# Loads of tiles 2 to 5 on the stores' DMA queue, in a kernel that scales every row by two weights

## The chip, the cores and the metric

The kernel runs on one core of a Trainium2 chip. The metric is the device time of one execution in microseconds (us); a kernel is run several times and the median is given. A profile is one further execution, recorded by the hardware profiler. DVE is VectorE, ACT is ScalarE, SP is SyncE, POOL is GpSimd. SP and ACT each have a DMA queue; both queues are served by the core's 16 DMA engines.

## What is computed

Each of 16 x 1024 tokens has a row of 512 floats and two weights. The output holds the row twice, each time multiplied by one of the weights:

```python
batch, seq, hidden, n_experts = 16, 1024, 512, 8     # k = 2
x_expanded = x[:, :, np.newaxis, :].repeat(k, axis=2)
weights = expert_weights[..., np.newaxis]
return (x_expanded * weights).astype(np.float32)
```

`expert_indices` is not used. 33.6 MB are read and 67.1 MB written.

## The kernel before

The 16384 tokens are cut into six tiles: five of 24 tokens for each of the 128 partitions, and one of 8 (`groups`, L33). In a tile, a partition holds successive tokens, so a load of a large tile is 128 rows of 48 KB (6144 KB), and tile 5's load is 2048 KB. `x_pool` has two buffers for loaded tiles, and so load i needs the buffer of tile i - 2. The output of a tile is made in halves of 12 tokens (`TO`), each in one of two buffers of `o_pool` and stored with one DMA of 6144 KB (L137). The text calls the two stores of tile i "ia" and "ib"; tile 5 has only one store, of 4096 KB.

The loop at L93 goes over the tiles. Of each six tokens of a half, four are multiplied by one DVE instruction (L121, 128 x 4096) and two by four ACT instructions (L104, 128 x 512 each). The first half of tile 0 is different: it is done row by row (L110 on DVE, L104 on ACT), because tile 0 is loaded in six chunks of four tokens (L81) so that work can start early.

`load(i)` (L75) issues the DMA of a tile. Loads 0 and 1 are issued ahead of the loop; load i + 2 is called at the end of the loop's turn for tile i (L141), so in program order it stands right behind that tile's last store. The stores are all issued from SP (L137). Which engine issues a load is chosen at L83: SP for the last tile, ACT for all others. An engine works through its program in order, and a DMA issue first waits for the semaphores it needs: a store for DVE and ACT to have written its half, a load for both engines to have read the old tile out of its buffer. The framework adds the semaphore waits; each DMA has one of eight completion semaphores in rotation, and it may also wait for the earlier transfer that used the same one. The weights (L54 to L60) come in three small loads on SP at the start.

Of the kernel before, what the change touches and what calls it, by code (L numbers as in the profile page):

```python
# [1 line left out]

# [4 lines left out]


@with_exitstack
def kernel(  # L10
    ctx: ExitStack,
    tc: tile.TileContext,
    x: bass.AP,
    expert_indices: bass.AP,
    expert_weights: bass.AP,
    out: bass.AP,
):
    nc = tc.nc

    batch, seq, hidden = x.shape  # L20
    k = expert_weights.shape[-1]
    P = nc.NUM_PARTITIONS
    ntok = batch * seq
    assert ntok % P == 0
    A_TOTAL = ntok // P

    f32 = mybir.dt.float32
    row = k * hidden
    TX = 24
    TO = 12  # L30
    CH = 4

    groups = [[24], [24], [24], [24], [24], [8]]  # L33
    assert sum(sum(g) for g in groups) == A_TOTAL

    xf = x.rearrange("b s h -> (b s) h")
    of = out.rearrange("b s k h -> (b s) (k h)")
    wf = expert_weights.rearrange("b s k -> (b s) k")

    w_pool = ctx.enter_context(tc.tile_pool(name="w_pool", bufs=1))  # L40
    x_pool = ctx.enter_context(tc.tile_pool(name="x_pool", bufs=2))
    o_pool = ctx.enter_context(tc.tile_pool(name="o_pool", bufs=2))

    w_tile = w_pool.tile([P, A_TOTAL * k], f32)

    def rows(of_all, done, T):
        return of_all[done * P : (done + T) * P, :].rearrange(
            "(p a) n -> p (a n)", a=T
        )

    T0 = sum(groups[0])
    G = len([g for g in groups[1:] if sum(g) == T0])
    head = (1 + G) * T0
    nc.sync.dma_start(out=w_tile[:, : T0 * k], in_=rows(wf, 0, T0))  # L54
    nc.sync.dma_start(
        out=w_tile[:, T0 * k : head * k].rearrange("p (g n) -> p g n", g=G),
        in_=wf[T0 * P : head * P, :].rearrange("(g p a) n -> p g (a n)", g=G, p=P),
    )
    nc.sync.dma_start(
        out=w_tile[:, head * k :], in_=rows(wf, head, A_TOTAL - head)  # L60
    )

    tiles = []
    done = 0
    for group in groups:
        T = sum(group)
        a0 = 0
        for n in group:
            tiles.append((done, T, a0, n))
            a0 += n  # L70
        done += T

    loaded = []

    def load(i):  # L75
        if i >= len(tiles):
            return
        done, T, a0, n = tiles[i]
        x_tile = x_pool.tile([P, TX * hidden], f32)
        src = rows(xf, done, T)  # L80
        step = TX // 6 if i == 0 else n  # L81

        queue = nc.sync if i == len(tiles) - 1 else nc.scalar  # L83
        for at in range(0, n, step):
            queue.dma_start(
                out=x_tile[:, at * hidden : (at + step) * hidden],
                in_=src[:, (a0 + at) * hidden : (a0 + at + step) * hidden],
            )
        loaded.append(x_tile)

    for i in range(2):
        load(i)
    for i, (done, T, a0, n) in enumerate(tiles):  # L93
        x_tile = loaded[i]
        outr = rows(of, done, T)
        for t in range(n):
            if t % TO == 0:
                o_tile = o_pool.tile([P, TO * row], f32)
            single = i == 0 and t < TO
            for kk in range(k if single or t % TO % 6 > 3 else 0):  # L100
                c = (done + a0 + t) * k + kk
                o = t % TO * row + kk * hidden
                if not single or c % 3 == 2:
                    nc.scalar.mul(  # L104
                        out=o_tile[:, o : o + hidden],
                        in_=x_tile[:, t * hidden : (t + 1) * hidden],
                        mul=w_tile[:, c : c + 1],
                    )
                    continue
                nc.vector.tensor_scalar(  # L110
                    out=o_tile[:, o : o + hidden],
                    in0=x_tile[:, t * hidden : (t + 1) * hidden],
                    scalar1=w_tile[:, c : c + 1],
                    scalar2=None,
                    op0=mybir.AluOpType.mult,
                )
            if not single and t % TO % 6 == 0:
                c = (done + a0 + t) * k
                o = t % TO * row
                m = min(CH, n - t)  # L120
                nc.vector.tensor_tensor(  # L121
                    out=o_tile[:, o : o + m * row].rearrange(
                        "p (t k h) -> p t k h", t=m, k=k
                    ),
                    in0=x_tile[:, t * hidden : (t + m) * hidden]
                    .rearrange("p (t h) -> p t h", t=m)
                    .unsqueeze(2)
                    .to_broadcast([P, m, k, hidden]),
                    in1=w_tile[:, c : c + m * k]
                    .rearrange("p (t k) -> p t k", t=m)  # L130
                    .unsqueeze(3)
                    .to_broadcast([P, m, k, hidden]),
                    op=mybir.AluOpType.mult,
                )
            if (t + 1) % TO == 0 or t + 1 == n:
                at = t // TO * TO
                nc.sync.dma_start(  # L137
                    out=outr[:, (a0 + at) * row : (a0 + t + 1) * row],
                    in_=o_tile[:, : (t + 1 - at) * row],
                )  # L140
        load(i + 2)  # L141

# [1 line left out]
_INS = ['x', 'expert_indices', 'expert_weights']  # L144
_OUTS = [((16, 1024, 2, 512), 'float32')]


# [23 lines left out]
```

## Time and profile before

| | |
|---|---|
| median of 3 runs | 240.34 us (240.26 to 242.69) |
| the profiled execution | 240.03 us, of which its span 238.1 us |
| DVE busy | 92.2 us (39%) |
| ACT busy | 54.2 us (23%) |
| moved by DMA | 100.80 MB, mean 423 GB/s over the span |
| large loads from ACT's queue | 4 of 6144 KB and 6 chunks of 1024 KB |
| stores from SP's queue | 10 of 6144 KB, 1 of 4096 KB |

The span runs from the first instruction to the last; the execution's own time has some 1.9 us around it. The profile cuts the span into 40 slices, and a digit is the busy share of a slice in tenths. An issue row of a DMA gives the time from issue to landing, that is until the last of its data has arrived and the semaphore is complete. A DMA queue on an engine is written SPq or ACTq. Row counts of x1 in the issue rows are single transfers, from the issues of a short stretch of time.

In the chain of work that ended last, stores hold 50% of the span, DVE's L121 18%, and loads 12%. The issue times of the kernel before: the stores 0b at 32.75, 1a 66.26, 1b 80.45, 2a 107.94, 2b 129.99, 3a 146.37, 3b 173.49, 4a 187.99, 4b 202.65 and 5 at 219.88 us; the loads 2 at 32.76, 3 at 80.47 and 4 at 130.01 us from ACT, and 5 at 173.92 us from SP.

### The profile page before, as it was taken

Reading aid. Unit: us, or ns where it says so; the run is one execution under the profiler, and the core shown is the slowest. Engines: PE = TensorE matmul, PEld = TensorE weight load, DVE = VectorE, ACT = ScalarE, POOL = GpSimd, SP = SyncE. Lnnn points to the kernel's source line nnn. Section 1 sums busy time; section 2 is a strip of 40 time slices with the busy share of each in tenths; the row PEclk is TensorE's granted clock in tenths of the full one; section 3 lists DMA queues with packets and bytes.
Section 4 is the critical chain, followed back from the end, with each engine's and each line's share of the span. In section 5 each row is a group of like instructions: output and inputs, shape, how many; then the busy total and the mean of one; then the engine's idle time right before and its main releaser. Section 6 shows DMA issues by size and latency. Waiting matters only on the chain.

```text
span 238.1 us, 232 instructions
## 1 busy us (share of the span) xinstructions
DVE 92.2 (39%) x36; ACT 54.2 (23%) x85; POOL 0.2 (0%) x4
## 2 busy tenths in 40 slices
DVE  0890240003919500391068085003919549019000
ACT  0841210003408000340061080003408044012000
POOL 0000000000000000000000000000000000000000
DMA  6998999999999999999999999999999999999996
GB/s 246 423 441 362 516 413 396 429 495 396 396 504 421 396 421 504 396 398 495 429 396 413 504 405 396 479 446 396 413 495 413 396 416 465 405 495 421 396 440 264
DMA packets 3986, 100.80 MB, mean 423 GB/s; under 512 B 1169, under 2 KB 1169, under 8 KB 1169
## 3 DMA queue, kind: packets, MB, share of 16 engines
q1 hardware_dynamic: 2544, 69.34, 67.5%
q10 hardware_dynamic: 1440, 31.46, 31.2%
q14 instruction: 2, 0.01, 0.0%
HBM read 33.69 MB, written 67.11 MB: 423 GB/s over the span
## 4 chain that ended last, share of the span: by engine, by line
DMA 62%; DVE 18%; another core or an unknown queue 10%; DVEq 1%; issue 0%; SPq 0%
DMA out_dram<-o_tile 50%; DVE o_tile L121 18%; DMA x_tile<-in_x_dram 12%; DVEq L166 1%; DVEq L121 0%; SPq L137 0%
## 5 line engine op out<-in xcount | busy, mean ns | idle before, releaser
L121 DVE TENSOR_TENSOR o_tile<-x_tile,w_tile 128x4096 f32<-128x4096 f32 (+1 forms) x20 | 85.6, 4316 | 121.0 <-DMA out_dram<-o_tile 85.7
L104 ACT ACTIVATE o_tile<-x_tile,w_tile 128x512 f32<-128x512 f32 x84 | 52.9, 709 | 155.0 <-DMA out_dram<-o_tile 115.8
L110 DVE TENSOR_SCALAR o_tile<-x_tile,w_tile 128x512 f32<-128x512 f32 x16 | 6.6, 483 | 6.6 <-DMA x_tile<-in_x_dram 6.6
L104 ACT ACT_TABLE_LOAD x1 | 1.3, 1283 | 6.6 <-DMA x_tile<-in_x_dram 6.6
L155 POOL MEMSET const-bfloat16-1.0<- 128x1 bf16 x1 | 0.1, 101 | 0.0
L155 POOL MEMSET const-uint8-127<- 128x1 uint8 x1 | 0.1, 101 | 0.0
L155 POOL MEMSET const-float32-0.0<- 128x1 f32 x1 | 0.1, 98 | 0.2 <-issue 0.2
L155 POOL MEMSET const-float32-1.0<- 128x1 f32 x1 | 0.1, 98 | 0.0
## 6 DMA issues: line engine op xcount, KB each, us to landing
out_dram<-o_tile SPq DMA_DIRECT2D x10, 6144.0 KB, 31.0
x_tile<-in_x_dram ACTq DMA_DIRECT2D x4, 6144.0 KB, 42.2
x_tile<-in_x_dram ACTq DMA_DIRECT2D x6, 1024.0 KB, 10.5
out_dram<-o_tile SPq DMA_DIRECT2D x1, 4096.0 KB, 17.4
x_tile<-in_x_dram SPq DMA_DIRECT2D x1, 2048.0 KB, 24.6
w_tile<-in_expert_weights_dram SPq DMA_DIRECT2D x1, 96.0 KB, 11.2
w_tile<-in_expert_weights_dram SPq DMA_DIRECT2D x1, 24.0 KB, 3.4
w_tile<-in_expert_weights_dram SPq DMA_DIRECT2D x1, 8.0 KB, 13.3
```

The lines of the kernel that those rows point to most:

```text
L104: nc.scalar.mul(out=o_tile[:, o : o + hidden], in_=x_tile[:, t * hidden : (t + 1) * hidden], mul=w_tile[:, c : c + 1],)
L110: nc.vector.tensor_scalar(out=o_tile[:, o : o + hidden], in0=x_tile[:, t * hidden : (t + 1) * hidden], scalar1=w_tile[:, c : c + 1], scala ...
L121: nc.vector.tensor_tensor(out=o_tile[:, o : o + m * row].rearrange("p (t k h) -> p t k h", t=m, k=k), in0=x_tile[:, t * hidden : (t + m) * ...
L155: nc = _bacc.Bacc("TRN2", target_bir_lowering=False, num_devices=1)
L166: with _tile.TileContext(nc) as tc:
```

## The change

Loads 2, 3 and 4 are issued from SP instead of from ACT, as load 5 already is. In SP's program each stands right behind the second store of the tile two before it, whose x buffer it takes. ACT's queue keeps the six chunks of tile 0 and the load of tile 1.

```diff
-        queue = nc.sync if i == len(tiles) - 1 else nc.scalar
+        queue = nc.sync if i >= 2 else nc.scalar
         for at in range(0, n, step):
             queue.dma_start(
```

Built, ACT's program loses three DMA issues and SP's gains them; SP's order becomes two stores, load, two stores, load, and so on. DVE's program has the same instructions in the same order.

## The prediction

> **What bounds the kernel now.** I read the page's table of slices first, then the DMA queues, then busy time by window, then the waits, then the single transfers.
>
> ```profile
> DMA  6998999999999999999999999999999999999996
> DMA packets 3986, 100.80 MB, mean 423 GB/s; under 512 B 1169, under 2 KB 1169, under 8 KB 1169
> q1 hardware_dynamic: 2544, 69.34, 67.5%
> q10 hardware_dynamic: 1440, 31.46, 31.2%
> ```
>
> The 16 DMA engines are 90% busy or more in nearly every slice. Only the first slice and the last are clearly lower. Packet time adds up to 67.5 + 31.2 = 98.7% of 16 engines' span: no spare DMA time exists, and the compute engines (DVE 39%, ACT 23%) are far from a bound. q10 is ACT's queue (the five large loads, 31.46 MB), q1 is SP's.
>
> The windows tell whether the mixture of loads and stores matters (columns: stretch, length, busy time and count for DVE, ACT and POOL, TensorE clock, DMA share, GB/s):
>
> ```profile
> 30.00:113.80 83.80, 28.97 (x7) 15.84 (x26) 0.00 (x0) 1.00 1.00 432
> 113.80:130.00 16.20, 8.76 (x2) 5.01 (x8) 0.00 (x0) 1.00 1.01 437
> 130.00:162.70 32.70, 8.76 (x2) 5.01 (x8) 0.00 (x0) 1.00 1.00 433
> 174.00:234.00 60.00, 24.15 (x6) 12.58 (x20) 0.00 (x0) 1.00 1.00 434
> 174.00:200.00 26.00, 14.93 (x4) 10.02 (x16) 0.00 (x0) 1.00 1.02 440
> ```
>
> In 30 to 113.8 and 130 to 162.7 a load on ACT's queue runs beside stores on SP's; in 113.8 to 130 there are stores alone; from 174 on, everything already sits in SP's one queue, with tile 5's load between two stores. The rate is 432 to 437 GB/s in all of them. What sets the time is therefore the bytes, and the DMA engines must merely never run out of queued work.
>
> ```profile
> ACT o_tile L104 <- DMA out_dram<-o_tile: 115.8, 8, 22.5
> DVE o_tile L121 <- DMA out_dram<-o_tile: 85.7, 8, 18.7
> DVE o_tile L121 <- DMA x_tile<-in_x_dram: 35.4, 3, 24.8
> ```
>
> DVE waits mostly for a store to give its o_tile back; it waited for loads three times only, and those are tiles 0 and 1.
>
> The issue rows by window give landing times, in order tile 0's second store, load 2, store 3b, load 5:
>
> ```profile
> out_dram<-o_tile SPq DMA_DIRECT2D x1, 6144.0 KB, 38.8
> x_tile<-in_x_dram ACTq DMA_DIRECT2D x1, 6144.0 KB, 51.8
> out_dram<-o_tile SPq DMA_DIRECT2D x1, 6144.0 KB, 20.2
> x_tile<-in_x_dram SPq DMA_DIRECT2D x1, 2048.0 KB, 24.6
> ```
>
> ```profile
> 173.92 0.82 SPq L85 DMA_DIRECT2D x_tile<-in_x_dram  x1
> 187.99 32.22 SPq L137 DMA_DIRECT2D out_dram<-o_tile  x3
> ```
>
> Store 3b is issued at 173.49 and lands at 173.49 + 20.2 = 193.7. Load 5, from SP, is issued at 173.92, so it did not wait for that store, and lands at 198.5, 4.8 us behind it. From there to the last landing (219.88 + 17.4 = 237.3) 18 MiB of load 5, stores 4a, 4b and 5 pass in 43.6 us: 14.53 us for each 6144 KB, or 433 GB/s. This is the unit of what follows.
>
> **The change, part by part.** Loads 2, 3 and 4 move from ACT's queue to SP's; load 5 was there and stays. No byte, arithmetic instruction or tile changes.
>
> *ACT loses three DMA issues* of 0.37, 0.36 and 0.35 us (1.08 us). ACT idles 155.0 us, so the gain on the path is 0.
>
> *SP gains three issues.* Load 5 shows 0.82 us for one issued right behind a store: 3 x 0.82 = 2.5 us. SP's stores wait 201.8 us for DVE in all, and the next store is over 25 us away in each case, so this is covered: 0. Without that cover it would be +2.5 us.
>
> *Waits on SP.* A load needs both engines to have finished with its x_tile; the store just ahead of it in SP's program waits for those same last instructions, so nothing new is waited for there. In the built program's list of waits, load 2 waits for tile 0's chunk loads, load 3 for load 1, load 4 for load 2 and store 0a, load 5 for load 3 and store 1a. All of these have landed long before by the schedule below. Queued behind the waiting load is the next tile's first store, which is not ready until later anyway. 0.
>
> *Order in the queue.* This is the real change: a load no longer shares the engines with stores but takes its turn. Up to 57.24 us (load 1 landed, the chain's row for L121 at 57.43) nothing differs, as load 2 sat behind load 1 so far. In the kernel before, store 0b then shared half the rate with load 2 until 32.75 + 38.8 = 71.5; alone it needs half of those 14.3 us and lands near 64.4. Counted backwards from 237.3 by bytes (11 units and 14.5 us for load 5 and store 5, 174.3 us) it is 63.0. I use 63.0, the one with less slack. Landings then follow each other by 14.53: load 2 at 77.5, store 1a 92.1, 1b 106.6, load 3 121.1, 2a 135.6, 2b 150.2, load 4 164.7, 3a 179.2, 3b 193.8, load 5 198.6, 4a 213.1, 4b 227.7, store 5 237.3. Before, 3a landed at 146.37 + 32.7 = 179.1: from there on both schedules are the same.
>
> Is each transfer issued before the one ahead of it ends? Half a tile takes 8.77 us on DVE (two of L121) plus about 0.1 us of issue. Store 1a is issued at 66.3 as before, 11.2 us before load 2 ends. Half 1b no longer waits for store 0b: issue at 75.0, 17 us ahead, and load 3 right behind it, 31 us ahead. Half 2a starts when 1a lands (92.1), issue 101.0 against 121.1: 20 us. Half 2b: 115.5 against 135.6. Half 3a: 144.5 against 164.7. Half 3b: 159.1 against 179.2. Half 4a: 188.1 against 198.6; 4b: 202.7 against 213.1; store 5: 219.8 against 227.7, 7.9 us. That smallest slack is in the kernel before too (219.88 against 202.65 + 24.9 = 227.6). The queue never empties, so the stall removed is 0 and the stall added is 0.
>
> *Loads landing later.* Load 3 lands at 121.1 instead of 80.47 + 33.3 = 113.8, load 4 at 164.7 instead of 162.7. Their tiles' first halves wait for a store's o_tile until 135.6 and 179.2, so 14.5 us of cover remain. DVE's waits just change length.
>
> *The turn from store to load inside one queue* is six times new. Between bounds: in the mixed stretches packets of both kinds alternate throughout, at 433 against 437 GB/s for stores alone; charged wholly to the turns, 0.9% of a 48 KB packet (128 rows of 48 KB over 16 engines are 8 packets, 14.53 / 8 = 1.8 us) is 0.02 us each, 0.1 us in sum. The other end is the 440 of 174 to 200, the very pattern in one queue: over the 117 us from 63 to 180 it would save 117 x 7 / 440 = 1.9 us. Its DMA share is 1.02, though, and 440 / 1.02 = 431: whole packets counted at the window's edge. I take 0.
>
> The Trainium skill's page "DMA: Bandwidth & Descriptors", section "Issuing engines are not separate DMA queues", says that transfers started from different engines run on the same 16 DMA engines and only issue time is saved by spreading them. By that rule the sum is 0 as well, and the rates by window agree. A rule that speaks against the change is in "Perfetto Trace Analysis" of the Trainium skill, section "DMA Optimizations": give inputs one issuing engine and outputs another, for a more dynamic spread. It is priced as the second rival; the 434 GB/s from 174 on, with both kinds in one queue, does not bear it out.
>
> **Sum.** 238.1 us span + 0 = 238.1; the profiled execution's own time is 240.03, 1.9 us more than its span, and the median of the runs shown is 240.34, 0.3 above it. Against that median: 240.3 us.
>
> **Rivals.**
>
> 1. *SP stalls at a load (slower).* If a load's issue had to wait for the store ahead of it to land, the one queue would run dry each time. The small 24 KB weight load shows 3.4 us from issue to landing, mostly start-up. Three or four such holes are +10 to +14 us, near 252. It decides where the awaited transfer lands later than the queue's last one. Against it: load 5 was issued 0.43 us after store 3b in the trace, 19.8 us before that landed, and the list of waits above names only old transfers.
> 2. *Head-of-line blocking (slower).* A finished first-half store stands behind a load in the queue, its o_tile comes back late, and a half's computing (8.8 us) is exposed in three tiles: up to +26 us, near 266. It decides once a store's issue is later than the end of the load ahead, that is when 11 to 20 us of slack are gone. Against it: 1a lands at 92.1 rather than at 66.26 + 32.7 = 99.0, since it no longer shares.
> 3. *One kind at a time is really quicker.* 240.3 - 1.9 = 238.4, from the 440 GB/s row; still within 1%. Over 1% would take 2.4 us, and the DMA share of 1.00 in the mixed stretches leaves no idle time to win. Against it as above.
>
> **How the numbers follow.** No change 0.87; rival 1 0.05; rival 2 0.03; rival 3 0.05, of which 0.02 over 1%. So faster by over 1% (which is about what a measurement of this kernel can tell from no change) 0.02, within 1% 0.87 + 0.03 = 0.90, slower 0.05 + 0.03 = 0.08. The range need not reach to the rivals, which hold 0.13. Low end: 434 instead of 432 GB/s over 117 us is -0.5 us, from the profiled 240.03: 239.5. High end: the turns' 0.1 us and the scatter, one of three runs at 242.69; half way from the median to it is 241.5.
>
> **What would show it.** Right: DMA 9 in all slices but the first and last; ACT's queue at 12.58 MB instead of 31.46; loads 2 to 4 issued within 1 us behind a second store, at about 33, 76 and 116, and load 5 at 160; load 3 landing near 121; 3a onward as before; a rate of 432 to 437 in each window; DVE's waits for loads still three. Wrong: a slice with DMA at 8 or less between 60 and 180 us, an SP load whose issue comes near the landing of the store ahead of it (rival 1), DVE waiting for x_tile beyond tile 1 or a store issued after its predecessor has landed (rival 2), or a longer steady rate near 440 (rival 3).

## The result, and the profile after

| | before | after |
|---|---|---|
| median of 20 runs | 240.36 us (239.88 to 243.5) | 242.17 us (240.21 to 243.01) |
| ratio of the times | | 1.0048, 95% interval 1.0026 to 1.007 |
| the profiled execution | 240.03 us, span 238.1 | 242.16 us, span 240.2 |

The change costs about half a per cent: 0.0048 x 240.36 = 1.15 us, between 0.6 and 1.7. The medians lie further apart (1.8 us) because both kernels scatter over about 3 us: of the 20 runs, 4 of the kernel before and 11 of the changed one are above 242 us. The two profiled executions, 2.1 us apart, show what separates such runs: that of the kernel before is one of its quickest, that of the changed kernel lies at its median.

The page of the changed kernel, with the DMA share by slice and the queues:

```profile
DMA  7999999999999999999999999999999999999993
DMA packets 3985, 100.80 MB, mean 420 GB/s; under 512 B 1168, under 2 KB 1168, under 8 KB 1168
q1 hardware_dynamic: 2976, 88.21, 85.4%
q10 hardware_dynamic: 1008, 12.58, 12.8%
```

The loads moved as written (ACT's queue q10 has 12.58 MB left), and no slice in the middle falls below 9. Only the last slice tells anything: 3 where it was 6. The windows of the changed kernel, with the columns as before:

```profile
30.00:113.80 83.80, 35.50 (x9) 20.59 (x33) 0.00 (x0) 1.00 1.00 431
130.00:162.70 32.70, 17.52 (x4) 10.02 (x16) 0.00 (x0) 1.00 1.00 433
174.00:234.00 60.00, 24.15 (x6) 12.58 (x20) 0.00 (x0) 1.00 1.00 431
```

The mean rate is at most 3 GB/s lower than in the same windows of the kernel before. The loss must be looked for in single transfers. Their issue rows in the changed kernel, one short window each, in this order: store 0b (issued at 32.48), load 2 (33.01), store 1b (74.67), load 3 (75.05), stores 2a (101.17) and 2b (115.75), load 4 (116.17), stores 3a (145.57) and 3b (160.01), load 5 (160.43), store 4a (189.71). Store 1a, between load 2 and store 1b, is left out. The last column is the time from issue to landing.

```profile
out_dram<-o_tile SPq DMA_DIRECT2D x1, 6144.0 KB, 30.7
x_tile<-in_x_dram SPq DMA_DIRECT2D x1, 6144.0 KB, 44.7
out_dram<-o_tile SPq DMA_DIRECT2D x1, 6144.0 KB, 32.1
x_tile<-in_x_dram SPq DMA_DIRECT2D x1, 6144.0 KB, 47.0
out_dram<-o_tile SPq DMA_DIRECT2D x1, 6144.0 KB, 35.4
out_dram<-o_tile SPq DMA_DIRECT2D x1, 6144.0 KB, 35.3
x_tile<-in_x_dram SPq DMA_DIRECT2D x1, 6144.0 KB, 50.1
out_dram<-o_tile SPq DMA_DIRECT2D x1, 6144.0 KB, 35.2
out_dram<-o_tile SPq DMA_DIRECT2D x1, 6144.0 KB, 35.3
x_tile<-in_x_dram SPq DMA_DIRECT2D x1, 2048.0 KB, 40.2
out_dram<-o_tile SPq DMA_DIRECT2D x1, 6144.0 KB, 25.5
```

Issue plus landing gives 63.2, 77.7, 106.8, 122.1, 136.6, 151.1, 166.3, 180.8, 195.3, 200.6, 215.2. So from one landing to the next: load 2 14.5 us, load 3 15.3, 2a 14.5, 2b 14.5, load 4 15.2, 3a 14.5, 3b 14.5, load 5 5.3, 4a 14.6. Every store takes 14.5 or 14.6, and so does load 2, which loses nothing. Loads 3 and 4 take 0.8 and 0.7 more, and load 5, of a third of the size, 0.5 more than its 4.8 in the kernel before. These three come to 2.0 of the 2.1 us between the two executions.

A landing is the last of 16 DMA engines. How far apart they are is seen at the very end, when nothing is queued any more. The kernel before (windows of 1 us):

```profile
235.00:236.00 1.00, 0.00 (x0) 0.00 (x0) 0.00 (x0) 1.00 1.06 459
236.00:237.00 1.00, 0.00 (x0) 0.00 (x0) 0.00 (x0) 1.00 0.01 0
```

and the changed kernel:

```profile
235.00:236.00 1.00, 0.00 (x0) 0.00 (x0) 0.00 (x0) 1.00 1.21 524
236.00:237.00 1.00, 0.00 (x0) 0.00 (x0) 0.00 (x0) 1.00 0.23 98
237.00:238.00 1.00, 0.00 (x0) 0.00 (x0) 0.00 (x0) 1.00 0.15 66
```

A packet counts in the window where it starts. In both kernels most engines begin their last packet before 236 us. Store 5's packets have 32 KB (4096 KB in 128 rows). In the changed kernel three of them begin between 236 and 237 us (98 GB/s for 1 us) and two between 237 and 238 (66). Most engines are as early as ever; a few are 1 to 2 us late, and the kernel waits for them.

The packet records of the two traces, which the views above only sum up, tell where those engines fall behind. Each trace has 1792 packets of 48 KB, and nearly all take 1.82 us. Over 0.1 us longer take 6 in the kernel before and 25 in the changed kernel. Of these 25, 14 begin from 118.1 to 119.4 us, in the last 4 us of load 3, and four from 162.7 to 163.6, in the last 4 us of load 4. The other seven begin in the first 5 us of loads 2, 3 and 4. So packets stretch near the places where loads and stores meet, most of them near the end of a load that has a store behind it.

### The profile page after: what moved, and what is told of

It is laid out like the page before. It is cut to its first block, busy times and chain, and to the rows that moved or that the text cites. A ratio compares the mean times of both kernels' runs of the same rounds, so it can differ in the third digit from the quotient of the medians.

```text
span 240.2 us, 237 instructions
## 1 busy us (share of the span) xinstructions
DVE 92.1 (38%) x36; ACT 54.2 (23%) x85; POOL 0.2 (0%) x4
## 3 DMA queue, kind: packets, MB, share of 16 engines
q10 hardware_dynamic: 1008, 12.58, 12.8%
## 4 chain that ended last, share of the span: by engine, by line
DMA 62%; DVE 18%; another core or an unknown queue 10%; DVEq 1%; issue 0%; SPq 0%
DMA out_dram<-o_tile 51%; DVE o_tile L121 18%; DMA x_tile<-in_x_dram 11%; DVEq L166 1%; DVEq L121 0%; SPq L137 0%
## 5 line engine op out<-in xcount | busy, mean ns | idle before, releaser
L104 ACT ACTIVATE o_tile<-x_tile,w_tile 128x512 f32<-128x512 f32 x84 | 52.9, 709 | 157.1 <-DMA out_dram<-o_tile 118.1
```

The costliest lines, as they stand in the source:

```text
L104: nc.scalar.mul(out=o_tile[:, o : o + hidden], in_=x_tile[:, t * hidden : (t + 1) * hidden], mul=w_tile[:, c : c + 1],)
```

## Experiments

Theory A said that a load which has the DMA engines to itself loses time on some of them, because no other queue's packets fill in; B, that reading by all engines at once loses time whatever the queues; C, that the turn between loads and stores inside one queue does; D, that it is an issue or arithmetic going on during the load; N, that it was chance.

**The changed kernel again**, unaltered.

> The changed kernel once more, unaltered, for a second trace. In the first trace load 3, load 4 and load 5 took 15.3, 15.2 and 5.4 us from the landing ahead of them, where stores of the same size took 14.5. Theory A (a load that has the DMA engines to itself loses time on a few engines, because no other queue's packets fill in): loads 2 to 4 together take 44.6 to 46 us between landings, the stores 14.5 each, time 0.3 to 0.9% above the kernel before. Theory C (the cost is of the turns from store to load in a queue): much the same. Rival N (chance, a disturbance of that one execution): loads 14.5 to 14.6 as well, time within 0.2% of the kernel before.

Measured 242.84 us, ratio 1.0061 (1.0036 to 1.0086). N falls. In this trace, too, all the stores behind load 2 take 14.5 or 14.6 us, while loads 3 and 4 take 15.4 and 16.0 and load 5 takes 5.1; load 2 takes 14.6. At the end the DMA share is 0.31, 0.08 and 0.15 in the windows from 236, 237 and 238 us.

**Loads alone and stores alone.** The edit is shortened here; one small store follows the loads.

```diff
+    for i in range(14):                      # x_pool with three buffers
+        x_tile = x_pool.tile([P, TX * hidden], f32)
+        queue = nc.sync                      # second: nc.scalar if i % 2 else nc.sync
+        queue.dma_start(out=x_tile[:, :], in_=rows(xf, i % 5 * TX, TX))
```

> Left out: weights, arithmetic and all stores but one small one. 14 loads of 6144 KB from SP's queue alone, three buffers, so that two further loads are always queued. 14 x 14.53 = 203.4, and with the start and the small store some 208 us of span if loads run like stores. Theory A (loads alone lose for want of a second queue): 4 to 10 us more than that, 0.3 to 0.7 per load. Theory B (reading alone by all engines at once loses time, whatever the queues): 4 to 10 us more as well. Theory C (turns from store to load cost): nothing more, within 1 us of 14.53 each.

> Left out: as in the kernel with loads from one queue. The same 14 loads, alternately from SP's and ACT's queue, so that mostly two are in flight at once. Theory A: 3 us or more shorter than from one queue, near 208 us of span. Theory B: as long as from one queue, within 1.5 us. Theory C: near 208 us, like one queue.

> Left out: all loads and the arithmetic; two filled buffers are stored 14 times with 6144 KB each from SP's queue. All theories: 14.5 us for each, 203 us and the start (filling the buffers, some 10 to 15 us): the measure of a transfer that loses nothing.

Loads from one queue took 212.06 us (span 210.4), from two queues 212.00 (210.2), stores 221.55 (219.8). The span of the loads is 2 us above the 208 forecast without a loss, short of the 4 to 10 that A and B expected, and the two kernels differ by 0.06 us. In one queue each load from the second on lands 14.5 us after the one ahead of it. The rate of loads in one queue, and then that of stores:

```profile
30.00:205.00 175.00, 0.00 (x0) 1.00 1.00 433
```

```profile
30.00:205.00 175.00, 0.00 (x0) 0.00 (x0) 1.00 1.00 431
```

Loads among loads lose no more than stores among stores. So A and B fall: it takes loads and stores together.

**Turns in one queue**, with nothing else. Two filled buffers are stored and loads go to buffers that nobody reads; only the order differs (the edit is shortened). In the built program the first load stands ahead of the first store, as the expectations write the order.

```diff
+    for what in "SSL" * 5:                   # then "S" * 10 + "L" * 5, then "SL" * 7
+        if what == "S":
+            nc.sync.dma_start(out=outr[:, ...], in_=o_tiles[stores % 2][:, :])
+        else:
+            queue.dma_start(out=x_tile[:, :], in_=rows(xf, loads % 5 * TX, TX))
```

> Left out: weights and arithmetic; two filled buffers are stored and loads go to buffers that nobody reads. Ten stores and five loads of 6144 KB, all from SP's queue, in the order L SS SS L SS L SS L SS L: eight turns between loads and stores. Theory C (a turn within one queue costs the slower engines some time; the changed kernel's two traces give 0.6 us for the two turns of a load, from 1.5 to 1.6 us for the three large ones and 0.3 to 0.6 for load 5): 1.8 us more than the kernel with two turns (6 x 0.3). Theory D (what costs is an issue or arithmetic going on during the load): the same time as with two turns, within 0.4 us.

> Left out: as above. The same ten stores and five loads from SP's queue, in the order L, ten S, four L: two turns. All theories: 14.5 us for each transfer between landings, and the span of the other less what six turns cost.

> Left out: weights and arithmetic, as in the kernels with eight and two turns. Seven stores and seven loads of 6144 KB, all from SP's queue, in the order L S S L S L S L S L S L S L: twelve turns, five loads in the middle and one at the end with stores ahead but none behind. Without any price of a turn the last landing is at 20.5 + 13 x 14.5 = 209.1 us. Theory C, as a price of each turn from load to store (the kernel with eight turns lost 0.2 to 0.7 at each of three middle loads and nothing at its last one): the five middle loads take 14.7 to 15.2 between landings, the last one 14.5, the last landing is at 210.1 to 212.6. If each turn from store to load costs too, the last load takes over 14.7 as well. Rival N (chance): all 14.5 to 14.6.

Measured 227.16 us with eight turns, 226.21 with two, 213.44 with twelve (that one moves one transfer less). With the same transfers, three more loads between stores cost 227.16 - 226.21 = 0.95 us, or 0.32 each, about half of the 1.8 us that C had forecast; the four runs of each kernel lie from 226.95 to 227.59 and from 225.31 to 226.37. For twelve turns the two-turn kernel less one transfer gives 226.21 - 14.5 = 211.7; the 1.7 us above it are 0.35 for each of five loads between stores. The issue rows with eight turns: the second store of the second pair (issued at 27.59), the first load between stores (28.32), the next store (29.05), the one after (29.78), the next load (30.53):

```profile
out_dram<-o_tile SPq DMA_DIRECT2D x1, 6144.0 KB, 50.7
x_tile<-in_x_dram SPq DMA_DIRECT2D x1, 6144.0 KB, 65.0
out_dram<-o_tile SPq DMA_DIRECT2D x1, 6144.0 KB, 78.9
out_dram<-o_tile SPq DMA_DIRECT2D x1, 6144.0 KB, 92.7
x_tile<-in_x_dram SPq DMA_DIRECT2D x1, 6144.0 KB, 106.6
```

Landings at 78.3, 93.3, 108.0, 122.5, 137.1: the first load takes 15.0 us, the second 14.6, the stores 14.5 to 14.7. With twelve turns the end is instructive: the last load between stores (issued at 122.90), a store (123.29), and the last load, which has a store ahead and nothing behind (152.30):

```profile
x_tile<-in_x_dram SPq DMA_DIRECT2D x1, 6144.0 KB, 58.4
out_dram<-o_tile SPq DMA_DIRECT2D x1, 6144.0 KB, 72.6
x_tile<-in_x_dram SPq DMA_DIRECT2D x1, 6144.0 KB, 58.0
```

Landings at 181.3, 195.9 and 210.3: the last load takes 14.4 us. In the two-turn kernel the loads behind the last store take 14.5 each (180.1, 194.6, 209.1, 223.6). So a load behind a store loses nothing as such; one that has a store behind it loses 0 to 1.2 us, differently each time (the five with twelve turns take 15.3, 15.7, 14.5, 14.9, 14.5). The first load of the two-turn kernel gives way to a store too. It lands at 20.5 us, the first of the loads alone at 18.6: 1.9 us, so the 0.32 and 0.35 are means and not a fixed price. C holds, as a price of the place where a load gives way to a store. D falls: while the loads between stores ran, there was no arithmetic, and SP issued nothing.

**More and fewer turns in the kernel.** First the x tiles in halves, so that a load of 3072 KB stands behind each store:

```diff
-    x_pool = ctx.enter_context(tc.tile_pool(name="x_pool", bufs=2))
+    x_pool = ctx.enter_context(tc.tile_pool(name="x_pool", bufs=4))
...
-        load(i + 2)
+                load(i + 2, t // TO)         # behind each half's store
```

> The changed kernel with the x tiles cut in two: a load of 3072 KB stands behind each first store and each second store, so the moved bytes are the same and the turns in SP's queue are twice as many for loads 2 to 4. Theory C: its loss over the kernel before is about double that of the changed kernel, 1.0% against 0.5% (near 242.7 against 241.5 where the kernel before has 240.3). Theory D (issues during a load) and any price per byte loaded: like the changed kernel, 0.3 to 0.7%.

Measured 243.03 us, ratio 1.008 (1.0049 to 1.011). That is 1.9 us for six loads between stores, 0.32 each: C's side, though the interval reaches down to 0.5% and so does not exclude by itself the 0.3 to 0.7% of D and of a price per byte.

Then load 5 on ACT's queue as well, and load 3 alone on SP's:

```diff
-        queue = nc.sync if i >= 2 else nc.scalar
+        queue = nc.scalar                    # second: nc.sync if i in (3, 5) else nc.scalar
```

> The kernel before with load 5, too, on ACT's queue: no queue turns any more. Theory C: nothing lost at load 5, whose two turns cost the kernel before next to nothing in its trace (4.8 us between landings): 0 to 0.2% below the kernel before. Rival (more mixing costs): slower by up to 0.3%.

> The kernel before with load 3 alone moved to SP's queue; loads 2 and 4 stay on ACT's. Theory C: load 3 stands between stores 1b and 2a in one queue and takes 15.0 to 15.4 us between landings; time 0.1 to 0.3% above the kernel before. Rival N (chance, or a cost of something else in the change): load 3 takes 14.5 to 14.6; the time as before, within 0.1%.

Measured 241.04 us, ratio 0.9987 (0.9955 to 1.0019), and 242.22 us, ratio 1.0017 (0.9986 to 1.0048). Both are too small for their intervals: they agree with 0.3 to 0.4 us for a load, and with nothing. In the second, load 4 from ACT's queue runs into the end of load 3, so that load 3's landing says nothing either.

Then the moved loads in four DMAs each, in the kernel and in the queue of eight turns:

```diff
-        step = TX // 6 if i == 0 else n
+        step = TX // 6 if i == 0 else n // 4 if i >= 2 else n
```

> The changed kernel with each moved load cut into four DMAs of a quarter of the row (12 KB rows for loads 2 to 4, 4 KB for load 5), the turns in SP's queue as many as before. If the price goes with the packet that is under way at the turn (48 KB, 1.8 us): a quarter of the loss, 0.1 to 0.3% above the kernel before. If it goes with the turn itself: 0.4 to 0.7% as for the changed kernel.

> Left out: weights and arithmetic. The kernel with eight turns in one queue (227.2 us, against 226.2 with two turns), each load cut into four DMAs of 12 KB rows. Price by packet: the middle loads 14.5 to 14.7 us from landing to landing, 226.0 to 226.5 us. Price by turn: 14.7 to 15.2, 226.9 to 227.6 us.

Measured 242.40 us, ratio 1.0042 (1.0016 to 1.0069), and 228.67 us. The kernel's loss is like that of whole loads, but its interval reaches into both forecasts. The bare queue became 1.5 us slower, outside both forecasts, so the smaller rows have a price of their own there. That the price goes with the packet under way is neither borne out nor excluded.

**The kernel before again.**

> The kernel before once more, for a second trace and for the scatter of its times. If the loss belongs to loads and stores in flight together, in one queue or in two: its runs fall again in two groups, about 240.4 and 242.4, and a trace of the slower group shows some DMA engines working 2 to 3 us after the others at the end. If only a turn within a queue can cost: all traces end within 1 us, whatever the time. Ratio 1 within 0.3%.

Ratio 0.9984 (0.9955 to 1.0013). The profiled execution took 242.86 us, 2.8 us more than that of the first trace, so this trace shows one of its longer runs. Store 3a, issued at 147.33, and then store 3b (175.25) and load 5 (175.69):

```profile
out_dram<-o_tile SPq DMA_DIRECT2D x1, 6144.0 KB, 33.5
```

```profile
out_dram<-o_tile SPq DMA_DIRECT2D x1, 6144.0 KB, 20.0
x_tile<-in_x_dram SPq DMA_DIRECT2D x1, 2048.0 KB, 25.7
```

Store 3a lands at 180.8 (179.1 in the first trace), so 1.7 us had gone by then, with all of loads 2 to 4 beside stores in the other queue. Load 5 takes 201.4 - 195.3 = 6.1 us instead of 4.8. The end is frayed as in the changed kernel:

```profile
236.00:237.00 1.00, 0.00 (x0) 0.00 (x0) 0.00 (x0) 1.00 0.23 98
237.00:238.00 1.00, 0.00 (x0) 0.00 (x0) 0.00 (x0) 1.00 0.08 33
238.00:239.00 1.00, 0.00 (x0) 0.00 (x0) 0.00 (x0) 1.00 0.08 33
```

Of its 1792 packets of 48 KB, 16 take over 0.1 us longer than 1.82. So the loss is not peculiar to one queue. Two queues can lose as much; here they do so in some executions, the changed kernel in most: over all sessions 37 of 113 runs of the kernel before and 23 of 32 of the changed one are above 242 us.

**What two queues cost.** The bare transfers of the eight-turn kernel, with the loads on ACT's queue.

```diff
-            queue = nc.sync
+            queue = nc.scalar
```

> Left out: as above. The same transfers with the loads on ACT's queue, beside the stores. Theory C: as short as with two turns, within 0.4 us, since no queue turns. Theory D: the same as both others.

Measured 244.00 us: 17 to 18 us more than in one queue, which no theory had. A try with the stores 10 us later followed.

> Left out: as before. The two-queue kernel of ten stores and five loads took 244 us where one queue took 226 to 227, its loads and stores running in step from the first store on. Here the stores start 10 us later (the second buffer filled is stored first), so that a store meets a load part of the way through it, as in the kernel before. Theory P (the loss comes from loads and stores that run in step): 227 to 231 us, the window of mixed transfers at 425 GB/s or more. Rival H (mixing in two queues costs in any case, here as there): 240 us or more.

It took 244.33 us, but the order of the two fillings changed nothing in time: its first store is issued at 13.68 us again. It tells nothing. Three further kernels use one buffer for both stores, filled by one instruction (first store at 26.48 us), by two (13.68), and by two with a first load of half the size:

```diff
-    nc.vector.memset(o_tile[:, :], 1.0)
+    nc.vector.memset(o_tile[:, : TO * row], 1.0)
+    nc.vector.memset(o_tile[:, TO * row :], 1.0)
```

> Left out: as before. Loads on ACT's queue, stores on SP's, the first store at about 24 us instead of 13.7 (one filling of 20 us for both buffers), in the middle of load 1. Theory P (bare transfers lose where loads and stores run in step): 225 GB/s of each kind at 425 GB/s or more in the mixed windows, some 230 us for the whole. Rival H (mixing two queues costs there in any case): 375 to 405 GB/s in the mixed windows, 240 us or more.

> Left out: as before. As the kernel whose stores start in the middle of a load, but the buffer is filled by two instructions, so that the first store starts 10 us earlier, where load 1 begins. Theory P (in step): 240 to 246 us and 375 to 405 GB/s in the mixed windows. Rival H2 (the single buffer made the difference): 225 to 227 us.

> Left out: as before. As the control, but the first load has half the size (3072 KB), so that the second load is some 7 us under way when the stores start: two to four of its eight packets per engine ahead. 7.3 us less to move than in the others. Theory P: 217 to 219 us, mixed windows at 425 GB/s or more. If the late start itself decided: 233 us or more.

Measured 224.87, 244.60 and 218.00 us. The windows from 40 to 110 us, where loads and stores are mixed, in the first, second and third:

```profile
40.00:110.00 70.00, 0.00 (x0) 0.00 (x0) 1.00 1.01 437
```

```profile
40.00:110.00 70.00, 0.00 (x0) 0.00 (x0) 1.00 1.00 379
```

```profile
40.00:110.00 70.00, 0.00 (x0) 0.00 (x0) 1.00 1.01 437
```

P holds: with a store starting in the middle of a load, two queues run at 437 GB/s. With loads and stores in step, each pair landing within 0.2 us of each other, they run at 379. In the packet records of these windows 256 of 540 packets take over 0.1 us longer than 1.82 us at 379 GB/s, and none of 622 in the first kernel. The first kernel is also 1.3 us quicker than one queue with two turns; its first load, with no store near, lands at 18.5 us instead of 20.5. The third kernel starts its stores as early as the second and runs like the first, so the start itself does not decide. In the kernel before a store is issued in the middle of a load (0b at 32.75, with load 1 landing at 57.2).

## Why the prediction was wrong, point by point

- **The time.** The forecast was 240.3 us, between 239.5 and 241.5; 242.17 was measured. That the change would stay within 1% (0.90) came true, with 0.48%, and slower rather than unchanged.
- **The bound was right.** The DMA engines stay 90% busy or more in all slices between the first and the last, and neither DVE nor SP became a limit.
- **ACT's and SP's issues, and the waits on SP: right, 0.** The loads are issued at 33.01, 75.05, 116.17 and 160.43 us; forecast were about 33, 76, 116 and 160. None waited for the store ahead of it (load 3: 0.38 us behind 1b's issue, 1b landing 32 us later). Rival 1 did not come.
- **The order of landings: right, up to the 2 us lost.** Load 3 at 122.1 (121.1), 1a at 66.00 + 26.2 = 92.2 (92.1). "3a onward as before" failed: it landed at 180.8 instead of 179.0. So did "432 to 437 in each window": the rate is 428 GB/s from 113.8 to 130 us. DVE still waits for loads three times, and every store is issued ahead of its turn. Rival 2 did not come either.
- **"The turn from store to load inside one queue": here it failed.** I put the six turns between +0.1 and -1.9 us and took 0. They cost 0.6 to 1.7 us, best 1.15, or 0.38 for each of the three moved loads, where the bare queues show 0.32 and 0.35; singly it was nothing for load 2 and 0.7 to 1.5 us for loads 3 and 4 in the two traces. The upper bound came from the wrong rows. It took every packet of the mixed stretches for a turn and so priced one at 0.02 us. And the rate by window is a mean over 16 engines: 432 against 431 GB/s from 63 to 180 us hides that a few of them fall behind while the end waits for the last. The name has the wrong side as well: it is mostly where a load gives way to a store that time is lost, not where it follows one.
- **The row from 174 to 200 us was one draw.** I read from load 5's 4.8 us that such a place is free. The same place of the same kernel took 6.1 us in its second trace.
- **The rule that speaks against the change.** The Trainium skill, "Perfetto Trace Analysis", section "DMA Optimizations", says that it may make sense to give inputs one issuing engine and outputs another. The sign agrees with the 0.48% here; its reason, a more dynamic spread, no run here shows. In the bare transfers the same separation cost 17 to 18 us where loads and stores ran in step. The other rule that I cited from the Trainium skill ("DMA: Bandwidth & Descriptors", section "Issuing engines are not separate DMA queues": the same 16 engines, only issue time saved) makes 0 of it, and the runs differ from that, by 0.5% here and by 379 against 437 GB/s in the bare transfers.
- **The base.** 240.3 us for the kernel before stands (240.36 with twenty runs), but the range's upper end came from three runs. With twenty, a fifth lie above 242; in the later sessions a third do, and its medians there are 241.2 to 241.9.

What stays open is why a DMA engine falls behind at such a place: the packets there take longer on some engines (by up to 0.65 us of 1.82 in the changed kernel's first trace), but the records do not tell whether the memory or the engine's own queue holds them. Also open is why the kernel before loses in some executions only.

## What to carry to other kernels

A mean DMA rate near its ceiling does not say that order is free: the end is set by the last of 16 engines, so look at the landings one by one and at how the share dies away in the last microseconds. A load set between stores in one queue cost some 0.35 us in the mean here (0 to 1.5 singly), small against its 14.5, and worth knowing only where nothing else is left. Price a new pattern from several executions of it, since one clean row may be luck.

## What the runs showed of the hardware

- Loads among loads (433 GB/s; one queue or two) and stores among stores (431; one queue) run alike; behind the start, loss came only where both kinds met. A packet of 48 KB takes 1.82 us, and 6 to 34 of 1792 in four traces of the two kernels take over 0.1 us more.
- Two queues whose loads and stores of 48 KB rows run in step kept losing for the whole of the mixture: 379 GB/s against 437 with the store in the middle of a load, 244.6 against 224.9 us for the same bytes. Half a load's shift is enough to undo it (218.0 us for 7.3 us less to move).
- The DMA share is 1.00 in the window at 379 GB/s as well as in those at 433: it counts the time of packets, and slow packets fill it just as well.
